# Exchanging the quadrants of a matrix by DMA alone: the transfers on two hardware queues instead of one

## The chip, the cores and the metric

The kernel runs on one core of one Trainium2 chip. The metric is the device time of one execution in microseconds (us). Each time is a median of several runs; lower is better.

## The reference

```python
def reference(x: np.ndarray) -> np.ndarray:
    return np.fft.ifftshift(x)      # x: 8192 x 8192, float32
```

For an even size, ifftshift moves every element by half the size in both directions, around the edge. So the output's upper left quadrant is the input's lower right one, the upper right is the lower left, and so on: four quadrants of 4096 x 4096 change places, and no value is computed. 268.4 MB are read and 268.4 MB are written.

## The kernel before, in words

The kernel copies from the input in device memory to the output in device memory, by DMA alone; nothing passes through a compute engine or through on-chip memory. The helper `both` (lines 25 to 34) issues one transfer. It covers 64 rows of the output (`rows`, 16 DMA engines times `apart` = 4 rows, lines 37 to 39) and in each row two pieces of 2048 floats (`piece`, 8 KB, line 38): one in the left half and one at the same place in the right half. The source is 4096 rows away, around the edge (line 31), and for the left piece it is the right half of the source row, for the right piece the left half: the second dimension of the source goes back by half a row (`-hc`, line 32), while that of the output goes forward (line 28). So one transfer is 64 x 2 pieces of 8 KB, 1 MB. A row is 32 KB; an engine has four rows of the 64, so two neighbouring engines work 128 KB apart.

The loops (lines 40 to 42) go over the 8192 rows in blocks of 64, and for each block over two column positions, `col` = 0 and 2048: the first and then the second quarter of both halves. That makes 128 x 2 = 256 transfers, all issued from the sync queue (SP), in the order of the output's rows. The framework deals out eight completion semaphores to the transfers in turn. A transfer waits, before it is issued, for the one that had its semaphore before, so at most eight are in flight. On each DMA engine a transfer is eight packets of 8 KB and one small write that counts up the semaphore.

Device memory has no other user here, and no other engine has work: the few instructions of line 57 on GpSimd are set-up.

Of the kernel before, what the change touches and what calls it, by code (L numbers as in the profile page):

```python
# [1 line left out]

# [4 lines left out]


ENGINES = 16  # L10


@with_exitstack
def kernel(
    ctx: ExitStack,
    tc: tile.TileContext,
    x: bass.AP,
    out: bass.AP,
):
    nc = tc.nc  # L20
    R, C = x.shape
    hr = R // 2
    hc = C // 2

    def both(queue, row, col, rows, piece):

        queue.dma_start(
            out=bass.AP(out.tensor, out.offset + row * C + col, [[C, rows], [hc, 2], [1, piece]]),
            in_=bass.AP(
                x.tensor,  # L30
                x.offset + (row + hr) % R * C + hc + col,
                [[C, rows], [-hc, 2], [1, piece]],
            ),
        )


    apart = 4
    piece = hc // 2
    rows = ENGINES * apart
    for row in range(0, R, rows):  # L40
        for col in (0, piece):
            both(nc.sync, row, col, rows, piece)


# [1 line left out]
_INS = ['x']  # L46
_OUTS = [((8192, 8192), 'float32')]


def kernel(**inputs):  # L50
    import numpy as _np
    import concourse.bacc as _bacc
    import concourse.tile as _tile
    from concourse import mybir as _mybir
    from concourse.bass_utils import run_bass_kernel_spmd as _run

    nc = _bacc.Bacc("TRN2", target_bir_lowering=False, num_devices=1)  # L57
    arrays, args = {}, []
    for name in _INS:
        a = _np.ascontiguousarray(inputs[name])  # L60
        if a.dtype.kind in "iu":
            a = a.astype(_np.int64)
        arrays[f"in_{name}_dram"] = a
        args.append(nc.dram_tensor(f"in_{name}_dram", a.shape, _mybir.dt.from_np(a.dtype), kind="ExternalInput").ap())
    for i, (shape, dtype) in enumerate(_OUTS):
        dt = _mybir.dt.from_np(_np.dtype(dtype))
        args.append(nc.dram_tensor(f"out_{i}_dram", shape, dt, kind="ExternalOutput").ap())
    with _tile.TileContext(nc) as tc:
        kernel(tc, *args)
    r = _run(nc, [arrays], core_ids=[0])  # L70
    got = tuple(r.results[0][f"out_{i}_dram"] for i in range(len(_OUTS)))
    return got[0]
```

## Time and profile before

| | before |
|---|---|
| median of 3 runs | 811.06 us (810.09 to 811.13) |
| the profiled execution's own time | 810.44 us |
| its span in the profile | 808.7 us |
| transfers, packets | 256 transfers, 36,864 packets in the sync queue |
| share of the 16 DMA engines | 99.3% |
| moved | 268.45 MB, mean 332 GB/s; 664 GB/s read and written together |
| busy compute engines | none but GpSimd, 0.2 us |

The profile page has a row for DMA that cuts the span into 40 slices of equal length: the digit is the busy share of the 16 DMA engines in tenths, and below it stands the rate in GB/s that they moved, counted once for a copy. "SPq" is the sequencer of the sync engine, which issues the transfers; its waits are the time in which it could not issue the next. "To landing" is the time from the issue of a transfer to its completion. The record of the trace also holds each single DMA packet with its start, duration and size; where a text speaks of packet records, it is these. The difference between the execution's time and its span, 1.7 us, lies around the span.

### The profile page before, as it was taken

The page shows a single profiled execution, that of the slowest core. Times are in us where ns is not written, and L with a number is a line of the kernel's source. Part 1 is how long each engine was busy: PE and PEld are TensorE (multiplying, and loading weights), DVE is VectorE, ACT ScalarE, POOL GpSimd, SP SyncE. Part 2 cuts the span into 40 slices and gives each one's busy share as a digit, 9 for nine tenths or more (in the row PEclk, how much of TensorE's full clock was granted, in tenths as well). Part 3 has the DMA queues.
Part 4 walks back from the last instruction along what each step waited for, and adds up shares of the span by engine and source line. Part 5 has one row for each costly group of instructions (what it writes and reads, how often), then busy time and mean ns, then how long its engine had stood idle before and what let it go on. Part 6 is the DMA issues. An engine that isn't in the chain of part 4 may idle for free. (4 is left out here: it accounts for less than half of the span.)

```text
span 808.7 us, 301 instructions
## 1 busy us (share of the span) xinstructions
POOL 0.2 (0%) x4
## 2 busy tenths in 40 slices
POOL 0000000000000000000000000000000000000000
DMA  8999999999999999999999999999999999999998
GB/s 301 331 335 329 336 334 330 335 332 336 332 335 334 336 331 334 339 328 335 331 335 339 334 334 337 331 336 330 336 334 331 339 332 334 333 336 331 337 335 294
DMA packets 36866, 268.47 MB, mean 332 GB/s; under 512 B 4096, under 2 KB 4096, under 8 KB 4096
## 3 DMA queue, kind: packets, MB, share of 16 engines
q1 hardware_dynamic: 36864, 268.45, 99.3%
q14 instruction: 2, 0.02, 0.0%
HBM read 268.44 MB, written 268.44 MB: 664 GB/s over the span
## 5 line engine op out<-in xcount | busy, mean ns | idle before, releaser
L57 POOL MEMSET const-bfloat16-1.0<- 128x1 bf16 x1 | 0.1, 102 | 0.0
L57 POOL MEMSET const-uint8-127<- 128x1 uint8 x1 | 0.1, 102 | 0.0
L57 POOL MEMSET const-float32-1.0<- 128x1 f32 x1 | 0.1, 99 | 0.0
L57 POOL MEMSET const-float32-0.0<- 128x1 f32 x1 | 0.1, 98 | 0.2 <-issue 0.2
## 6 DMA issues: line engine op xcount, KB each, us to landing
out_dram<-in_x_dram SPq DMA_DIRECT2D x256, 1024.0 KB, 25.1
```

Source lines behind the costliest of these rows:

```text
L57: nc = _bacc.Bacc("TRN2", target_bir_lowering=False, num_devices=1)
```

## The change

The loop over rows goes over the upper 4096 rows of the output only. In each step the sync queue gets the transfer as before, and the scalar queue (ACT) gets one of the same shape for the block 4096 rows further down. The number, size and shape of the transfers stay the same, 256 of 1 MB; 128 of them are now issued from each queue, and the order in which the output's blocks come up is another.

```diff
-    for row in range(0, R, rows):
+    for row in range(0, hr, rows):
         for col in (0, piece):
             both(nc.sync, row, col, rows, piece)
+            both(nc.scalar, hr + row, col, rows, piece)
```

In the built program the eight completion semaphores are dealt out over both queues in turn, four to each. So each queue waits for its own transfer of four before, and again at most eight are in flight.

## The prediction

> **What bounds the kernel now.** I read the page first, then the waits, then the windows at both ends and in the middle, and last the records of the single packets. In the page I look for anything that is not the transfer itself.
>
> ```profile
> span 808.7 us, 301 instructions
> ...
> DMA  8999999999999999999999999999999999999998
> GB/s 301 331 335 329 336 334 330 335 332 336 332 335 334 336 331 334 339 328 335 331 335 339 334 334 337 331 336 330 336 334 331 339 332 334 333 336 331 337 335 294
> ...
> q1 hardware_dynamic: 36864, 268.45, 99.3%
> ```
>
> No compute engine works. The 16 DMA engines are busy 99.3% of the span, and only the first and the last slice fall off. The 38 slices between (20.2 us each) have a mean of 333.9 GB/s, with 328 as the lowest and 339 as the highest. So the time is the sum of packet times and nothing else, if the engines never run dry. The next two views test that: who waits, and what one issue costs.
>
> ```profile
> SPq L27 <- DMA out_dram<-in_x_dram: 634.0, 248, 3.2
> SPq L68 <- DMA out_dram<-in_x_dram: 24.1, 4, 15.2
> ```
>
> ```profile
> L27 SPq DMA_DIRECT2D out_dram<-in_x_dram x256: 562/562/682, 0.7 to 783.1; - x128
> ...
> DMA to landing us min/median/max: 6.0/25.1/26.0
> ```
>
> The sync queue waits 634.0 us, in 248 of 256 transfers, for a transfer that was issued eight before. It is far ahead of the engines: an issue takes 0.562 us, a transfer 805 / 256 = 3.14 us of engine time, and one is issued 25.1 us = 8 x 3.14 us before it lands. Issuing is not the limit.
>
> The packets: 99.3% of 16 x 808.7 us is 12,849 us of packet time. The 4096 completion writes take 9 ns each by their records, 37 us; that leaves 391 ns for each of the 32,768 packets of 8 KB. Their records say how this mean comes about: 62% take at most 320 ns (median 309), the other 38% take 523 ns on average. 309 ns is the floor of an engine; the 82 ns above it in the mean are contention, and they make 82 ns x 2048 packets per engine = 168 us of the time. Between packets there are some 3 to 4 ns. Those that follow a completion write directly have the same mean (390 ns, the 945 of them that can be told apart). So a transfer's end leaves no hole.
>
> **The change, part by part.**
>
> *Issue.* Sync issues 128 transfers instead of 256, scalar 128: 72 us of issuing on each instead of 144 us on one. The wait of 634.0 us shows that this is hidden; saving 0. In the built program scalar has nothing else to do than these transfers, so nothing is queued behind them.
>
> *Waits.* The eight completion semaphores are dealt out in turn over both queues, so in the built program each queue waits for its own transfer of four before, and eight are in flight as before. With an equal share, a transfer takes 6.28 us beside the other queue's, four of them again 25 us. The refill needs a landing to be seen and one issue of 0.56 us, while three transfers (19 us) still stand in that ring. The 16 completions of one transfer come within 0.7 to 3.0 us of each other (median 2.0), so the quickest engine is less than one transfer ahead. Cost 0; without that cover it would be an empty ring while the other ring still works, and so still nothing.
>
> *Both ends.* Windows (us, POOL busy and count, PEclk, DMA share, GB/s):
>
> ```profile
> 2.00:4.00 2.00, 0.00 (x0) 1.00 0.86 254
> 4.00:8.00 4.00, 0.00 (x0) 1.00 1.02 385
> 8.00:12.00 4.00, 0.00 (x0) 1.00 1.01 344
> ...
> 804.00:808.70 4.70, 0.00 (x0) 1.00 0.47 187
> ```
>
> The first packet starts at 2.2 us, 1.5 us after the first issue; a second queue doesn't make that earlier. The last engines end within some 3 us of each other; one more transfer beside the last changes this by no more than about 1 us either way. I take 0.
>
> *The packets.* This is what decides. The engines are the same 16, with no gaps, and the floor is theirs; only the 82 ns of contention can move. Now all engines work in one block of 64 rows at a time, reading it in x and writing it in the output, engines 128 KB apart. Afterwards each engine has two rings, one for each half of the output: two blocks of x are read and two of the output written, 128 MB apart. No row of this trace shows four blocks at once, so the price is bounded by rows from both sides. The highest rate is 437 GB/s in 0.3 us slices between 4 and 6 us, and the lowest, among 2.5 us slices, is here (100 to 200 us):
>
> ```profile
> GB/s 341 318 318 331 377 331 318 351 328 311 318 354 328 328 351 344 301 311 360 334 351 321 295 367 321 370 285 354 338 357 315 331 328 338 357 321 338 331 334 344
> ```
>
> Held throughout, 437 would give 805.2 x 333.9 / 437 + 5 = 620 us and 285 would give 948 us. These are moments; over 20.2 us nothing leaves 328 to 339. I take the nearest row, the long slices, as the scale of what different meetings of addresses do: the lower half of the 38 has a mean of 331.7 GB/s, the upper quarter 337.2.
>
> For the sign: when the engines have just set out together, they move 385 GB/s (4 to 8 us), then 344, then 334, while their spread in one transfer grows from 0.7 us to 2 us. The further apart they are, the more they meet. Two rings spread them further. Against that: from 20 us on the spread still grows from 1.0 to 2.0 us and the rate doesn't fall, so the effect is small. Hence the lower half of the slices: 805.2 us x (333.9 / 331.7 - 1) = +5.3 us. From the profiled execution's 810.4 us that is 815.7 us, and from the median of 811.06 us, 0.6 above it, 816.4. I say **816 us**.
>
> A row that speaks of pitch is missing here. The Trainium skill (DMA: Bandwidth & Descriptors, Latency and other measured facts) has copies slowed when streams stand at large powers of two apart: 207 GB/s at a pitch of 512 KiB, 103 at 4 and 8 MiB, and full rate, 214, with 4 KiB more. An estimate by that page, with its mildest ratio, is 811 x 214 / 207 = 838 us; the sum above does not use it.
>
> **The rivals.**
>
> *Same, 811 us.* No idle engine, no hole at a transfer's end, same packets, same eight in flight: contention is then a mean over many accidental meetings and stays 82 ns. For it: 334 GB/s from 20 to 408 us and 334 from 408 to 796 us, although the halves of the matrix are exchanged between. Against it: 20 us slices still differ by 3%, so where streams meet does matter. The Trainium skill (the same page, Issuing engines are not separate DMA queues) says that transfers of several queues run on the same 16 engines and that only issue time is saved; by that rule the time stays here, and the trace agrees in that issue time is hidden already.
>
> *Faster, 803 us.* One mechanism: two rings on one engine let a packet of the second ring start while one of the first is held up in memory. Its place is the 38% slow packets, its price the 523 - 309 = 214 ns that each loses. At 5% of these delays hidden, 0.05 x 168 = 8.4 us are gained, 802 us, which is about what the upper quarter of slices gives: 805.2 x (1 - 333.9 / 337.2) = 7.9 us, 803 us. It decides from the point at which packets overlap on an engine, so that the packet times exceed the 99.3%. For it: the memory takes 437 GB/s for moments, so 334 is no hard ceiling. Against it: the packets already follow each other within 4 ns, and all 16 engines share the memory that delays them.
>
> *Much slower, 837 us.* The two rings of an engine are exactly 128 MB apart in x and in the output, so every packet could meet its neighbour in the same parts of memory. If the share of slow packets grows from 38% to 44%, the mean grows by 0.06 x 214 = 12.8 ns, x 2048 = +26 us. For it: the two streams advance in step. Against it: reading and writing already go on at related addresses, and 62% of packets are at the floor.
>
> *The change doesn't do what it says:* if one queue gets a larger share of each engine, it ends early and the other runs the rest alone, with four transfers in flight, 12.5 us of work. That is the rate of now, so at most a part of the time is as forecast; it lies between "same" and the forecast.
>
> **How the numbers follow.** A little slower (816) 0.36, much slower (837) 0.11, same 0.20, faster (803) 0.33. Within 0.2%, what a measurement of this kernel can tell from no change, is 809.4 to 812.7. So faster 0.33, same 0.20, slower 0.47. The range: the highest long slice, 339, gives 805.2 x (333.9 / 339 - 1) = -12.1 us, 799 us; a little below that, at 797, about a third of the faster case is left out (0.11). Upward the lowest slice, 328, gives +14.5 us, 826 us, and half of the much slower case is to be taken in: 838, which leaves out some 0.07. As both signs are likely, the forecast's own range is 812.7 to 826.
>
> **What would show it.** Two queues of 18,432 packets each, together about 99%; a floor that stays at 309 ns; scalar and sync both waiting over 300 us for their own transfers, landing still near 25 us. If I am right, the middle slices have a mean near 331.7 GB/s and the slow packets are more, not longer gaps. Faster shows as slices above 336, by fewer slow packets or by packet times that overlap. The forecast is wrong in kind if the DMA share falls (an empty ring), if one queue ends long before the other, or if the first or last slice moves by more than 1 us of work.

## The result and the profile after

The changed kernel took 814.95 us (median of 6 runs, 814.80 to 816.22), the kernel before 811.48 us beside it (6 runs, 810.09 to 812.97). The ratio is 1.0042, 95% interval 1.003 to 1.0055: slower by 0.4%. The forecast was 816 us.

The page of the changed kernel (span, DMA busy tenths and GB/s in 40 slices, then packets, MB and share of the 16 engines by queue):

```profile
span 813.1 us, 301 instructions
...
DMA  8999999999999999999999999999999999999999
GB/s 300 329 330 337 330 332 332 332 334 331 332 330 330 336 329 331 333 331 331 333 331 332 330 333 331 331 331 329 335 331 331 332 332 332 332 329 337 332 330 302
...
q10 hardware_dynamic: 18432, 134.23, 49.5%
q1 hardware_dynamic: 18432, 134.23, 49.4%
```

The 38 middle slices have a mean of 331.7 GB/s, against 333.9 before, and reach only from 329 to 337. So the loss is spread over the whole run; no stage carries it. The two queues carry half each. Their shares sum to 98.9% where the one queue had 99.3%: the engines are idle for a little longer, by the packet records 8.6 of 813.1 us against 5.6 of 808.7 us.

The line that issues the transfers, and the sync queue's waits (us in total, times, longest):

```profile
L27 ACTq DMA_DIRECT2D out_dram<-in_x_dram x128: 570/570/672, 0.7 to 784.9; - x128
L27 SPq DMA_DIRECT2D out_dram<-in_x_dram x128: 562/562/833, 0.7 to 789.8; - x128
...
DMA to landing us min/median/max: 6.6/25.3/27.5
```

```profile
SPq L27 <- DMA out_dram<-in_x_dram: 714.9, 124, 8.3
```

A ring is the list of waiting packets that one queue has on one engine. Issuing is halved and hidden, and a transfer still lands 25.3 us after its issue: the rings are as full as before. The view shows no waits of the scalar queue, so only sync's half of that part of the forecast is seen.

The packet records separate the loss. A packet of 8 KB takes 391.7 ns on average, 0.7 ns more than before: x 2048 = 1.5 us. The floor is still 309 ns. The packets above 320 ns are more (43% instead of 38%) but shorter (502 ns instead of 523). Added up, packets fill 804.5 us of each engine (803.1 before), and the other 3.0 us of the 4.4 us that the span grew are idle time. This is a balance, because the records also overlap: in both kernels more than 16 packets of 8 KB are on record at once for about 9% of the time. An engine that stands empty isn't seen: apart from the first 8 us and the last 6 us, the mean number of packets on record falls in no stretch of 2 us below 15.2, and below 15.1 before. The completions of one transfer come within 1.1 us of each other (median; about 2.0 before), so in this profile the engines drift apart less.

How the rings are served is seen at the start. This is the view of the DMA queues for the first 12 us:

```profile
q10 hardware_dynamic: 279, 2.10, 50.6%
q1 hardware_dynamic: 182, 1.36, 32.0%
```

The scalar queue (q10) is ahead. By the packet records the engines take their first packets from it alone; the first of sync's starts 2.6 us later. From 10 us behind the first packet, where the engines stand in step, the share of the scalar queue in stretches of 0.4 us goes 69, 31, 71, 31, 69, 31, 67, 33%: each engine takes one packet from each ring in turn. That holds for the whole run: there are 30,219 pairs in which a packet of 8 KB starts 3 or 4 ns before another ends, and in 95% of them the two are of different queues. (Packets of other engines meet it so by chance, some 1,300 pairs for each ns, half of them of one queue; that is about the rest.) The completions of the scalar queue are ahead of sync's by about six of its packets (median 5.9). The Trainium skill (DMA: Bandwidth & Descriptors, Queues, rings and completion order) says that an engine goes round the queues that have work, packet by packet, and gives a packet as typically 9 to 17 descriptors. The trace agrees with the taking of turns; here the turn changes after each piece of 8 KB, 391.7 ns in the mean.

### The profile page after: what moved, and what is told of

It reads as the page before. It is cut to its first block, busy times and chain, and to the rows that moved or that the text cites. A ratio compares the mean times of both kernels' runs of the same rounds, so it can differ in the third digit from the quotient of the medians.

```text
span 813.1 us, 301 instructions
## 1 busy us (share of the span) xinstructions
POOL 0.2 (0%) x4
## 2 busy tenths in 40 slices
DMA packets 36866, 268.47 MB, mean 330 GB/s; under 512 B 4096, under 2 KB 4096, under 8 KB 4096
## 6 DMA issues: line engine op xcount, KB each, us to landing
out_dram<-in_x_dram SPq DMA_DIRECT2D x128, 1024.0 KB, 25.3
```

## The experiments

Each ratio is against the kernel before, run on the same chip in turn. The chips differ: before took 821.96 us in the first set, 810.61 us in the second and 823.05 us in the third. So only ratios are compared across sets. The figures in brackets behind a ratio are its 95% interval. The first three edits are shown against the changed kernel, the others against the kernel before, if not said otherwise; `...` stands for lines left out.

Two theories stood at first. **Places** (theory A): the loss comes from working 128 MB apart. **Rings** (theory B): it comes from engines that take packets from two rings in turn. Others came from the runs.

### The change's order from one queue

```diff
-            both(nc.scalar, hr + row, col, rows, piece)
+            both(nc.sync, hr + row, col, rows, piece)
```

> All 256 transfers from the sync queue, in the changed kernel's order: a block of the upper half, the same block of the lower half, and so on. Theory A (places): the loss of the change comes from working in blocks 128 MB apart, so that even one queue that goes to and fro between them is slower than before, 1.002 to 1.004 of it, though less than the change, as an engine does eight packets in one half before it goes to the other. Theory B (rings): the loss comes from each engine taking packets from two rings in turn, so one queue in any order is as fast as before, 1.000 with no more than 0.002 either way, and its idle time of the DMA engines stays at 0.7% of the span. Theory C (order alone): it has the change's whole ratio, 1.004.

Measured 821.75 us, ratio 0.9998 (0.9989 to 1.0007). Going to and fro between places 128 MB apart, with every transfer, costs nothing. The order of the transfers alone is not the cause.

### Two queues in the same rows

```diff
-    for row in range(0, hr, rows):
-        for col in (0, piece):
-            both(nc.sync, row, col, rows, piece)
-            both(nc.scalar, hr + row, col, rows, piece)
+    for row in range(0, R, rows):
+        both(nc.sync, row, 0, rows, piece)
+        both(nc.scalar, row, piece, rows, piece)
```

> Two queues, but both in the same 64 rows: sync moves the first quarter of both halves, scalar the second quarter, 8 KB beside it. Theory A (places): nothing is far apart, so 1.000 of before, within 0.002, busy share 99.3%. Theory B (rings): the alternation of rings is as in the change, so 1.004 of before (815 us), with a busy share near 98.9%. Theory C (order alone): the order of addresses is that of before, 1.000.

Measured 825.55 us, ratio 1.0042 (1.0028 to 1.0055): the change's whole loss, without any distance. "Places" falls as the cause of the change's loss; "rings" holds so far. The page of this kernel:

```profile
q1 hardware_dynamic: 18432, 134.23, 49.6%
q10 hardware_dynamic: 18432, 134.23, 49.5%
```

The shares sum to 99.1%, and the packets' mean is 397.5 ns, against 396.0 ns of the one-queue kernel above, which was as fast as before on that chip. Of the 4.9 us by which the span is longer than that kernel's, 3.1 us are longer packets (1.5 ns x 2048) and the rest is idle time. In the change it was the other way round, 1.4 us and 3.0. So which of the two it is does not explain the loss.

### 128 MB plus or minus 8 KB

```diff
-            both(nc.scalar, hr + row, col, rows, piece)
+            both(nc.scalar, hr + row, piece - col, rows, piece)
```

> The change with one thing different: the scalar queue takes the two quarters in the opposite order, so the two streams stand 128 MB plus or minus 8 KB apart and not exactly 128 MB. If the exact power of two is what costs (a special case of theory A), it returns to 1.000 of before, within 0.002. Theory A without it, and theory B (rings): 1.004, as the change.

Measured 824.95 us, ratio 1.0037 (1.0024 to 1.0049). The exact power of two is not it. The Trainium skill (the same page, Latency and other measured facts) has streams 4 MiB apart back at full rate with 4 KiB of padding. In this run 8 KB changed the ratio from 1.0042 to 1.0037, each within the other's interval, so a rule of that kind between the two streams is not what slows this kernel.

### Four blocks from one queue

```diff
-            out=bass.AP(out.tensor, out.offset + row * C + col, [[C, rows], [hc, 2], [1, piece]]),
+            out=bass.AP(out.tensor, out.offset + row * C + col, [[C, rows], [hr * C, 2], [1, piece]]),
...
-        for col in (0, piece):
+        for col in (0, hc, piece, hc + piece):
```

(The source goes back by `hr * C` in its second dimension, the loop over rows goes over the upper half only, and all transfers are sync's.)

> One queue, and every engine goes from the upper to the lower half of the output from packet to packet, by one transfer that holds one quarter of 64 rows of both halves of the matrix (1 MB, 256 of them). Four blocks 128 MB apart are worked in at once, as in the change, but from one ring. Theory A (places): 1.004 of before, or more since the alternation is strict. Theory B (rings): 1.000 within 0.002 and a busy share near 99.3%. What is not the same as in the change: the two pieces of a row are moved by different transfers, about 3 us apart instead of 0.8.

Measured 825.17 us, ratio 1.0042 (1.0029 to 1.0054). That is against "rings": the loss is there with one ring. As it stands it would speak for "places", which the second kernel had ruled out. But the three slow sorts of kernel share something else: an engine's consecutive packets are no longer the two pieces of one row that exchange halves. From here I had another theory, **pairs** (theory D), and made the second set.

### One queue, one side at a time

```diff
-            out=bass.AP(out.tensor, out.offset + row * C + col, [[C, rows], [hc, 2], [1, piece]]),
+            out=bass.AP(
+                out.tensor,
+                out.offset + row * C + half * hc + piece,
+                [[C, rows], [-piece, 2], [1, piece]],
+            ),
```

(Source alike, in the other half; `half` 0 and 1 take the place of the two quarters, all from sync. This helper is called `one_side` below.)

> One queue, blocks in the order of before, 256 transfers of 1 MB, but a transfer covers the two quarters of one half of 64 rows (packets of 8 KB, second quarter first) instead of the same quarter of both halves. So an engine's next packet is 8 KB beside the last one and no longer the piece of the same row in the other half. Theory D (pairs): what the change, the two queues in the same rows and the four blocks from one queue have in common is that the two pieces of a row, which exchange their halves, no longer follow each other on an engine; by it this kernel loses the same, 1.004 of before. Theory A (places) and theory B (rings): nothing is far apart and there is one ring, so 1.000 within 0.002.

Measured 817.11 us, ratio 1.0091 (1.0076 to 1.0105): twice the change's loss, with one ring and nothing far apart. Its page, and below it that of the kernel before, profiled on the same chip:

```profile
span 815.3 us, 301 instructions
...
GB/s 287 322 329 328 324 326 329 329 333 326 338 329 330 331 333 332 334 332 335 326 337 329 334 336 330 336 332 337 334 338 330 327 330 337 335 324 335 328 332 297
...
q1 hardware_dynamic: 36864, 268.45, 99.2%
```

```profile
span 809.1 us, 301 instructions
...
GB/s 300 335 334 333 336 325 333 330 336 333 332 337 336 332 335 330 336 335 330 332 333 333 337 332 336 334 338 333 335 333 335 330 335 330 335 337 330 334 333 301
...
q1 hardware_dynamic: 36864, 268.45, 99.5%
```

The number, size and queue of the packets are the same, yet slices 2 to 8 stay under 330 (322 to 329) where before has 332 in the mean. Only the order of the packets is another. So this order by itself is worth up to 0.9%. The loss doesn't last, though the order does: slices 13 to 39 have a mean of 332.4, against 333.7 before.

### Two queues, one for each side

```diff
-        for col in (0, piece):
-            both(nc.sync, row, col, rows, piece)
+        one_side(nc.sync, row, 0, rows, piece)
+        one_side(nc.scalar, row, 1, rows, piece)
```

> Two queues in the same 64 rows, sync for the left half of the output and scalar for the right half, both taking the second quarter before the first. If an engine takes packets from its two rings in turn, the two pieces of a row follow each other again as in before, but from two rings. Theory D (pairs): 1.000 of before, within 0.002. Theory B (rings): 1.004, as with the other kernels on two queues.

Measured 811.82 us, ratio 1.0015 (1.0006 to 1.0023). Two rings, in turn on each engine, with packets that go from half to half again: two thirds of the loss are gone. What a second ring costs as such is about 0.15% in this kernel, 0.23% by the end of the interval. "Rings" falls as the main cause. But here the scalar queue is 2 packets ahead (its first packet starts 1.4 us before sync's), so the pieces that follow each other are not of the same row; that speaks for the halves and not the row.

### Longer pieces, and before once more

```diff
-        for col in (0, piece):
-            both(nc.sync, row, col, rows, piece)
+        both(nc.sync, row, 0, rows, hc)
```

> One queue as before, but the pieces are whole half rows of 16 KB, 128 transfers of 2 MB. If what matters is how often an engine goes from one place to another, half as many steps bring a gain: theory D or A would give 0.996 to 1.000 of before. Theory B (rings): 1.000. If longer packets meet more in memory, it is slower.

Measured 813.87 us, ratio 1.0038 (1.0026 to 1.0051): 16 KB packets are slower than 8 KB, so fewer steps do not help. It fits none of the theories' gains; the expectation's last sentence had this case, and why it is so was not followed up.

> The kernel of before unchanged, for its packet records and idle share on the same chip as the others: by every theory 1.000, busy share 99.3%, and the same mean packet time as the one-queue kernels of equal time.

Measured 810.88 us, once. The packets' mean is 392.1 ns, with less idle time than in the first profile of before: 3.8 us against 5.6 at nearly the same span. So the split into packet time and idle time wanders by about 2 us from profile to profile; the change's 3.0 us more of idle time, from one profile each, is not far beyond that. The engines' spread in one transfer wanders too: its median is 1.2 us here and was about 2.0 in the first profile, at the same speed.

### Two queues 128 MB apart, sides crossed, and uncrossed

```diff
+    for row in range(0, hr, rows):
+        for half in (0, 1):
+            one_side(nc.sync, row, half, rows, piece)
+            one_side(nc.scalar, hr + row, 1 - half, rows, piece)
```

> Two queues and the change's order of blocks, 128 MB apart, but while sync moves pieces of the left half, scalar moves pieces of the right half of its own block, and the other way round. So an engine that takes a packet from each ring in turn always goes from one half of a row to the other, though the rows are 4096 apart. Theory E (halves): what counts is only that consecutive packets of an engine lie in opposite halves, in whatever row; 1.000 to 1.002 of before, as two queues that share the two halves of the same rows. Theory D (pairs of one row): those pairs are gone, 1.004 or more. Theory A (places 128 MB apart): 1.004.

```diff
-            one_side(nc.scalar, hr + row, 1 - half, rows, piece)
+            one_side(nc.scalar, hr + row, half, rows, piece)
```

(against the crossed kernel)

> As the crossed kernel, but both queues move the same half at the same time, so that consecutive packets of an engine hardly ever change halves. Theory E (halves): about 1.009 of before, as the one queue that moves one side at a time. Theory A and theory D: the same as the crossed kernel, about 1.004.

Measured 821.29 us, ratio 0.9979 (0.997 to 0.9988), and 821.43 us, ratio 0.9976 (0.9966 to 0.9985): both are faster than before, and equal. The view of the queues for the first 12 us of the crossed kernel:

```profile
q10 hardware_dynamic: 276, 2.10, 51.3%
q1 hardware_dynamic: 176, 1.31, 31.0%
```

The scalar queue leads by six packets again, in both kernels, which my expectation had not counted. A transfer has eight packets on an engine, so for six of eight the scalar ring is already in the next transfer, and that has the other half. Consecutive packets lie in opposite halves for about a quarter of the time in the crossed kernel and about three quarters in the uncrossed one (the small completion writes are left out of this count). By the halves the two should differ, and the crossed one should be slow. Neither is so. Theory E, halves as the only thing that counts, falls for kernels on two queues whose blocks are far apart. "Places" has no room here either: at 128 MB apart two queues win 0.2%.

### Without the exchange of halves

```diff
-                x.offset + (row + hr) % R * C + hc + col,
-                [[C, rows], [-hc, 2], [1, piece]],
+                x.offset + (row + hr) % R * C + col,
+                [[C, rows], [hc, 2], [1, piece]],
```

> One queue and the order of before, but the halves of a row aren't exchanged: the left piece is read from the left half of the row 4096 away, the right one from the right half, so the output is shifted in rows only. Consecutive packets still lie in opposite halves, for reading and for writing. In before, the next packet is read from the same half that this packet is written to; here from the other one. Theory E1 (going from half to half as such is what helps): 1.000 of before. Theory E2 (what helps is that the next packet's source lies in the same half as this packet's destination): it loses that, 1.009.

Measured 829.23 us, ratio 1.0077 (1.0064 to 1.009).

```diff
-                x.offset + (row + hr) % R * C + (1 - half) * hc + piece,
+                x.offset + (row + hr) % R * C + half * hc + piece,
```

(in the kernel of one queue, one side at a time)

> One queue that moves one half at a time, as the one-side kernel, and the halves aren't exchanged either: the left half is read from the left half of the row 4096 away, so the output is shifted in rows only. Consecutive packets stay in one half, and the next packet's source lies in the same half as this packet's destination. Theory E1 (going from half to half as such is what helps): 1.009 of before. Theory E2 (source of the next in the half of this one's destination): 1.000.

Measured 824.84 us, ratio 1.0019 (1.0007 to 1.003).

The two swap their places against their counterparts with the exchange: the order that is fast there (1.000) is slow here (1.0077), and the slow one (1.0091) is nearly as fast as before (1.0019). So going from half to half as such does not help (E1 falls). What separates the one-queue kernels with 8 KB packets is E2: whether the next packet is read from the half in which this packet is written. It is so in before, in the alternating kernel and in the last one (0.9998 to 1.0019), and not so in the four blocks, the one side and the one without exchange (1.0042 to 1.0091). E2 was set down before the last two runs. It doesn't give the sizes: the four blocks lose half of what the one side loses, and the last one is a little slower than before (1.0019, 1.0007 to 1.003). Nor does it give the longer pieces, which follow it and take 1.0038.

The page of the kernel that keeps the two pieces and only leaves out the exchange (1.0077) shows something more:

```profile
span 828.2 us, 301 instructions
...
GB/s 288 324 315 325 314 321 315 325 316 317 320 319 321 324 330 326 336 330 332 331 327 331 332 326 336 329 328 332 330 327 335 327 324 329 329 325 330 325 323 292
```

Its order of packets is the same from start to end, but slices 2 to 12 have a mean of 319.2 GB/s and slices 13 to 39 one of 328.7. By its packet records a packet takes 407 to 414 ns as long as the 16 engines are within 0.7 to 1.0 us of each other in a transfer, in the first three tenths of the transfers, and 391 to 398 ns once they are 1.7 us or more apart. The one side goes the same way, from 406 ns at 1.1 us to some 392 at 2 us. So in these two the order costs much only while the engines are nearly in step, and one engine's neighbours alone don't set the loss. What the engines ask of memory at the same moment may have a part in it; the rows that are worked on change along the run as well, and no run here separates these.

## Why the prediction was right, and where its reasons were not

*Issue, waits, ends:* right. Issues of 0.562 and 0.570 us are hidden, landing stays at 25.3 us, the first slice moves from 301 to 300 GB/s and the last from 294 to 302, which is 0.5 us of work. The DMA share did fall, by 0.4 points, which the prediction had named as a sign of an empty ring; with landing at 25 us and no 2 us in which fewer packets are on record than before, none is seen here.

*The size:* right, but by luck. The middle slices were forecast at 331.7 GB/s and are at 331.7; the span grew by 4.4 us, forecast 5.3. (The 805.2 us of that sum isn't derived there; from the first packet to the last it is 805.4 us by the records.) It was priced by what the rate of the kernel before varies by itself over long slices. Nothing ties the mean of the lower half of these slices to what two queues do, and two queues in another order were 0.2% faster, which is the other sign of the same scale.

*The form of the loss:* wrong in part. More slow packets were forecast, "not longer gaps". There are more, but shorter ones, and 3.0 of the 4.4 us are idle time in the one profile. The reading of the gaps was wrong too: "some 3 to 4 ns" between packets is not what the records of the kernel before show. Mostly the next packet starts 3 or 4 ns before the last one ends (30,493 pairs among 32,768 packets), and the idle time lies elsewhere.

*The sign's reason:* wrong. The step "The further apart they are, the more they meet. Two rings spread them further" failed in both halves. The engines' spread in a transfer fell from about 2.0 to 1.1 us, and the kernel before is as fast at 1.2 us as at 2.0. In the one side and the one without exchange it is the other way round: packets are slowest while the engines are in step. Working 128 MB apart costs nothing either (0.9998 with one queue; 0.9979 and 0.9976 with two). The loss is there with both queues in the same rows (1.0042), and with one queue in other orders (1.0042, 1.0091). What the runs show in its place: the order of the packets. Packet by packet from two rings, about half of the neighbours in an engine's sequence lie in the same half of the matrix; before, none did. By E2 that is about half of the good neighbours lost, and the loss of 0.4% lies between none lost (1.000 to 1.002) and the larger of the losses with all lost (1.004 to 1.009). So E2 agrees with the change, the two kernels like it (1.0042, 1.0037) and the one with a queue for each side (1.0015, few or none lost). That it is the cause in the change is argued, not shown.

*What stays open:* E2 does not give the two fastest kernels, which lose three quarters and one quarter of the good neighbours and are both 0.2% faster. Between them and the kernel with a queue for each side stand the distance of the blocks and the ring's lead, which were not separated. So it is shown that the order alone, with the number, size and queue of the packets kept, moves the time from 0.9998 to 1.0091 of before. By which property of the addresses, and whether through one engine's neighbours or through engines in step, is not shown, and E2 is a rule of the one-queue kernels with 8 KB packets only. The traces hold no addresses either: the order within a transfer is read from the kernel's access patterns.

*The rivals:* "same" had the right reason that issue is hidden already, but left out that a second ring also changes the order. "Faster" had its place in the slow packets; 0.2% of gain does exist with two rings in another order, about a quarter of its 7.9 us. By what mechanism is not shown. Its sign, records that overlap on an engine, can't tell: they overlap in the kernel before as well. "Much slower" did not come; neither 128 MB nor 128 MB plus or minus 8 KB did what its 26 us needed.

## What to carry to other kernels

Where the DMA engines are full, as here, expect a second queue to reorder the packets of each engine more than to add bandwidth. In this copy orders and queues moved the time between 0.9976 and 1.0091; so write down the sequence of one engine, ring by ring, before arguing with distances. The variation of the old kernel's long slices (328 to 339 around 333.9 GB/s) took in all of these ratios, but it gave no sign. Look also at how the rate goes over the run: an order that stays the same and a loss that ends say that something else has a part. To find the cause, hold the queue and change the order, then hold the order and change the queue: either alone would have ended in a wrong theory here.

## What the hardware showed that was not expected

Sync's ring is not served from the start: the scalar ring had 2.6 us alone and kept about six packets of lead to the end; with a queue for each side it had 1.4 us alone and a lead of two. The same kernel differs by 1.5% between chips (810.61 and 823.05 us). The version that beats both kernels is two queues, each moving one side of its own half at a time: 0.9976 to 0.9979 of before.
